# Attention scores by pairs of query tiles, with the second term as two 64-row products in the array's halves

## The chip, the cores and the metric

The kernel runs on one core of one Trainium2 chip. The metric is device time in microseconds of one execution. The time before is the median of three runs. Five engines work side by side, each with its own queue in program order: PE (TensorE, the 128 x 128 array), DVE (VectorE), ACT (ScalarE), POOL (GpSimd) and SP (SyncE), which only issues transfers. They wait for each other by semaphores.

## The reference

One decoder block over 2048 tokens of width 1024, in float32. What matters here is the mixer's attention: eight heads of width 64, strictly causal, in query tiles of 128.

```python
z = jnp.einsum('bhqd,bhkd->bhqk', qb, kb) * inv_sqrt
mask = s_idx < t_idx
log1m = jnp.where(mask, -jax.nn.softplus(z), 0.0)
after = lax.cumsum(log1m, axis=3, reverse=True) - log1m
logw = jax.nn.log_sigmoid(z) + after
w = jnp.where(mask, jnp.exp(jnp.where(mask, logw, 0.0)), 0.0)
outs.append(jnp.einsum('bhqk,bhkd->bhqd', w, vb))
```

Around it stand a conditioning product, a norm, one input projection (q, k, v and the pooling channels u), a causal pooling mixer, the output projection, and a dense SwiGLU layer.

## The kernel before, in words

**Precision.** Each operand of a product is split into a high and a low part in the fast float32r type: `split` casts on ACT (L58) and subtracts on DVE or POOL (L59). A product is then the sum of the terms high x high, high x low and low x high (`mm3`, L68 to L70).

**Stages.** First conditioning and the first projections; then attention, into which the rest of the projections is woven; then the output projection (`mix`), and the dense layer to the end, which is PE's alone.

**The attention's units.** A unit is (head h, query block tb, key block sc), both blocks of 512 tokens. There are 8 x 10 = 80 units; 32 have sc = tb (the diagonal). A unit has 4 steps, one for each query tile i of 128. A diagonal unit's step covers L = (i + 1) x 128 keys, all others 512. So there are 320 steps, 192 of them with 512 keys in 48 full units.

**A step's work, in order.** `weights_step` multiplies the tile's queries with the keys into z, one of two banks z0 and z1. The tile `qt` holds q's high part in both halves of the 128 rows, and q's low part likewise; `kt` holds k's high part in rows 0 to 63 and its low part in rows 64 to 127. So one 128-row product with `qt[:, 0]` gives high x (high + low) (L795), a second with `qt[:, 1]` gives low x (high + low) (L796). ACT makes two sigmoids of z, sg (L798) and pr (L800). `scan_step` runs a product scan over pr on DVE from the right (L811, `begin` holds the masks) and multiplies sg by it on POOL to give w (L817), with small copies of the carry (L808 to L815). `turn_step` transposes a unit's four w by key block b on PE into a bank wt (L828), casts it on ACT (wth, L58) and subtracts on DVE (wtl, L59). `values_step` multiplies both parts with the values (L843, L844) into one bank `av`; at a query block's end ACT copies it out (o, L848) and SP stores it.

**What sets the order.** PE, ACT, DVE and POOL run in the order in which this Python loop issues; SP's order is set by the framework's scheduler. Iteration n of the loop does: `values_step` of the turn three iterations back (LAG); `weights_step` of step n; `scan_step`, one a turn of the loop, if more than one is listed in `scans`; `turn_step` of step n - 7 (OFF); then filler pieces, as many as a pace sets that counts 4.0 for a full step and 2.5 for a diagonal one. A filler piece is three products of a projection (L68 to L70); every ninth piece is empty. 192 of the 226 pieces lie in the attention stage. With `block_loads` SP loads a block's q, k and v tiles (L777 to L779).

Of the kernel before, what the change touches and what calls it, by code (L numbers as in the profile page):

```python
# [10 lines left out]
F32R = mybir.dt.float32r  # L11
# [6 lines left out]
P = 128  # L18
# [5 lines left out]
DH = 64  # L24
# [4 lines left out]
TB = 512  # L29
# [14 lines left out]
def block_kernel(ctx, tc, x, c, w_cond, b_cond, g_mix_pre, g_mix_post, w_in, w_pool,  # L44
                 pool_scale, w_out, g_ffn_pre, g_ffn_post, w_gate, w_up, w_down, out):
    nc = tc.nc
# [6 lines left out]
    def raw(ap):  # L53
        return ap.bitcast(F32)
# [17 lines left out]
    def open_pool(stack, name, bufs=1, side=None):  # L72
        kw = {"side": side} if side else {}
        return stack.enter_context(tc.tile_pool(name=name, bufs=bufs, reuse_waits="tile", **kw))
# [4 lines left out]
    def dt(name, shape):  # L79
        return dram.tile(shape, F32, tag=name, name=name)  # L80

    qd = [[dt(f"qd{i}_{tb}", [2, P, TB]) for tb in range(NTB)] for i in range(4)]
    kd = [[dt(f"kd{i}_{tb}", [2, P, TB]) for tb in range(NTB)] for i in range(4)]
# [68 lines left out]
    def bank_cycle(*tags):  # L152
        tags = itertools.cycle(tags)
        return lambda name: psum(next(tags), 1, name)

    z_ps, t_ps, av_ps, mm_only = bank_cycle("z0", "z1", "z2"), bank_cycle("w0", "w1"), bank_cycle("a0", "a1"), bank_cycle("mm")
# [608 lines left out]
    qkp = open_pool(ph1, "qk", bufs=2)  # L765
    kv = {}

    def block_loads(h, tb):
        hp, j = h // 2, h % 2
        r = slice(j * DH, (j + 1) * DH)  # L770
        kt = qkp.tile([P, TB], F32R, tag="kt", bufs=6, name=f"kt{h}_{tb}")
        vt = att.tile([P, 4, P], F32R, tag="vt", bufs=6, name=f"vt{h}_{tb}")
        kv[h, tb] = kt, vt
        qt = qkp.tile([P, 2, TB], F32R, tag="qt", name=f"qt{h}_{tb}")
        for l in range(2):
            half = slice(l * DH, (l + 1) * DH)
            nc.sync.dma_start(raw(qt[half]), qd[hp][tb][:, r, :].rearrange("l d t -> d l t"))  # L777
            nc.sync.dma_start(raw(kt[half]), kd[hp][tb][l, r, :])
        nc.sync.dma_start(raw(vt), vd[tb][:, h, :].rearrange("(b p) e -> p b e", p=P))  # L779
        return qt  # L780

    qts, carries, avs, wss = {}, {}, {}, {}

    scans = []

    def weights_step(u, i):

        h, tb, sc = u
        diag = sc == tb
        kt, qt = kv[h, sc][0], qts[h, tb]  # L790
        L = (i + 1) * P if diag else TB
        nm = f"{h}_{tb}_{sc}_{i}"
        z = z_ps(f"z{nm}")
        keys = kt[:, 0:L]
        nc.tensor.matmul(z[:, 0:L], qt[:, 0, i * P:(i + 1) * P], keys, start=True, stop=False)  # L795
        nc.tensor.matmul(z[:, 0:L], qt[:, 1, i * P:(i + 1) * P], keys, start=False, stop=True)  # L796
        sg = att.tile([P, TB], F32, tag="sg", bufs=5, name=f"sg{nm}")
        nc.scalar.activation(sg[:, 0:L], z[:, 0:L], AF.Sigmoid, scale=0.125)  # L798
        pr = att.tile([P, TB + 1], F32, tag="pr", bufs=PRB, name=f"pr{nm}")
        nc.scalar.activation(pr[:, 0:L], z[:, 0:L], AF.Sigmoid, scale=-0.125)  # L800
        scans.append((u, i, pr, sg, L, nm))

    def scan_step(u, i, pr, sg, L, nm):

        diag = u[1] == u[2]
        carry = carries.pop(i, None)
        if carry is None:
            nc.gpsimd.memset(pr[:, L:L + 1], 0.0)  # L808
        else:
            nc.gpsimd.tensor_copy(pr[:, L:L + 1], carry)  # L810
        nc.vector.tensor_tensor_scan(pr[:, 0:L][:, ::-1], pr[:, 0:L][:, ::-1], begin[:, TB - L:][:, ::-1],  # L811
                                     zero if carry is None else carry, ALU.mult, ALU.max if diag else ALU.bypass)
        if u[2]:
            carries[i] = att.tile([P, 1], F32, tag=f"carry{i}", bufs=2, name=f"carry{nm}")
            nc.gpsimd.tensor_copy(carries[i], pr[:, 0:1])  # L815
        w = att.tile([P, TB], F32, tag="w", bufs=OFF + 4, name=f"w{nm}")
        nc.gpsimd.tensor_tensor(w[:, 0:L], sg[:, 0:L], pr[:, 1:L + 1], ALU.mult)  # L817
        wss.setdefault(u, []).append(w)

    def turn_step(u, b):  # L820

        h, tb, sc = u
        i0 = b if sc == tb else 0
        lo0 = i0 * P
        nm = f"{h}_{tb}_{sc}_{b}"
        wt = t_ps(f"wt{nm}")
        for i in range(i0, 4):
            nc.tensor.transpose(wt[:, i * P:(i + 1) * P], wss[u][i][:, b * P:(b + 1) * P], ident)  # L828
        wh = att.tile([P, TB], F32R, tag="wth", bufs=4, name=f"wth{nm}")
        wl = att.tile([P, TB], F32R, tag="wtl", bufs=4, name=f"wtl{nm}")  # L830
        split(wh[:, lo0:], wl[:, lo0:], wt[:, lo0:])
        return wh, wl, lo0

    def values_step(u, b, wh, wl, lo0):
        h, tb, sc = u
        hp, j = h // 2, h % 2
        first = sc == tb and b == 0
        last = sc == 0 and b == 3
        if first:
            avs[h, tb] = av_ps(f"av{h}_{tb}")  # L840
        av = avs[h, tb]
        vb = kv[h, sc][1][:, b, :]
        nc.tensor.matmul(av[:, lo0:], vb, wh[:, lo0:], start=first, stop=False)  # L843
        nc.tensor.matmul(av[:, lo0:], vb, wl[:, lo0:], start=False, stop=last)  # L844
        if last:
            end = (h, tb) == (HEADS - 1, NTB - 1)
            o1 = (up if end else wsp).tile([P, TB], F32, tag="um" if end else "o1", bufs=1, name=f"o1_{h}_{tb}")
            nc.scalar.copy(o1, av)  # L848
            for part, dst in enumerate((mtd, mld)):
                (nc.scalar if end else nc.sync).dma_start(dst[tb][hp, j * DH:(j + 1) * DH, :], o1[part * DH:(part + 1) * DH])  # L850

    def unit_loads(u):
        h, tb, sc = u
        if sc == tb:
            qts[h, tb] = block_loads(h, tb)
# [29 lines left out]
    z_ps, t_ps, av_ps, mm_only = bank_cycle(*('z0', 'z1')), bank_cycle(*('w0', 'w1', 'a1')), bank_cycle(*('a0',)), bank_cycle(*('mm',))  # L885
    steps = [(u, i) for u in units for i in range(4)]

    def wo_load():
        nonlocal wo_next
        for l in range(2):  # L890
            nc.sync.dma_start(raw(wo[wo_next][l]), wod[wo_next][l])
        wo_next += 1
# [20 lines left out]
    def mix_add(T, m32, l32):  # L913
        nc.gpsimd.tensor_tensor(m32[:, 0:HK], m32[:, 0:HK], l32, ALU.add)
        return T, m32
# [9 lines left out]
    def mix_products(T, mh, ml):  # L925
        pss = []
        for nh in range(2):
            cs2 = slice(nh * TB, (nh + 1) * TB)
            pss.append(f_ps(f"mix{T}_{nh}"))
            for k in range(KC):  # L930
                mm3(pss[nh], [((mh[:, k, :], ml[:, k, :]), (wo[k][0][:, cs2], wo[k][1][:, cs2]))],
                    first=k == 0, last=k == KC - 1)
                yield
        mixed[T] = pss
# [16 lines left out]
    for n in range(len(steps) + OFF):  # L951
        if len(waiting) > LAG:
            values_step(*waiting.pop(0))
        if n < len(steps):
            u, i = steps[n]
            if i == 0:
                unit_loads(u)
            weights_step(u, i)
            spent += 2.5 if u[1] == u[2] else 4.0
        if len(scans) > 1 or n >= len(steps) and scans:  # L960
            scan_step(*scans.pop(0))
        if n >= OFF:
            u, b = steps[n - OFF]
            waiting.append((u, b, *turn_step(u, b)))
        goal = START + (N_PIECES - START) * spent / (4 * sum(area[:END]))
        while fill is not None and taken < goal:
            taken += 1
            if next(fill, 0) == 0:
                fill = None
        for pool, here in ((hb, not wo and taken >= HB_FREE), (ha, len(wo) == 4 and fill is None)):  # L970
            if here:
                hi, lo = (pool.tile([P, 4, D], F32R, tag=tag, name=f"wo_{pool.name}{tag}")
                          for tag in ("hi", "lo"))
                wo.extend((hi[:, k, :], lo[:, k, :]) for k in range(4))
        if wo_next < len(wo):
            wo_load()
        if n in FIRST_LOADS:
            firsts.append(mix_load(SEQUENCE[FIRST_LOADS.index(n)]))
        if n in FIRST_SPLITS:
            products.append(mix_products(*mix_split(*firsts.pop(0))))  # L980
        if n in FIRST_ADDS:
            firsts[0] = mix_add(*firsts[0])
        if n >= len(steps):
            mix_pieces(PER_STEP)
# [592 lines left out]
```

## Time and profile before

| | us |
|---|---|
| median of three runs | 2325.14 (2323.5 to 2328.67) |
| the profiled execution | 2330.08 |
| its span, first to last instruction | 2328.3 |
| attention stage, first score product to last scan | 323.6 to about 840 |

The mean granted TensorE clock is 0.990. A line of a view names the engine, the line of the program, the operation, what is written `<-` what is read, and the form. Starts and durations of PE overlap, since products are pipelined: the distance from start to start tells what one costs. In a list of waits the three numbers are the total in us, how often, and the longest.

### The profile page before, as it was taken

To read this page: it belongs to the slowest core of one execution; us is meant where nothing else is said; L and a number is where in the kernel's file an instruction comes from. 1 tells how busy PE (TensorE), PEld (TensorE's weight loads), DVE (VectorE), ACT (ScalarE), POOL (GpSimd) and SP (SyncE) were. 2 spreads that over 40 slices of the span, in tenths; PEclk is the share of its full clock that TensorE was granted. 3 is DMA by queue.
4 is the path that set the end of the run, shared out by engine and by line. 5 is a ranking of instruction groups with operands and counts; after the bars stand their busy time and mean duration, and the time that the engine had idled before them with its cause. 6 is when DMAs were issued, how large, how long until landed. Compare 5 with 4: busy or idle time off the path is not lost.

```text
span 2328.3 us, 33054 instructions
## 1 busy us (share of the span) xinstructions
PE 2260.6 (97%) x10589; PEld 1854.3 (80%) x10589; DVE 1629.2 (70%) x2222; ACT 1163.5 (50%) x2411; POOL 1317.6 (57%) x1619
## 2 busy tenths in 40 slices
PE   6999999999999999999999999999999999999997
PEld 4778778888888777887888888888888888888885
DVE  6764549999999966756666565887766556565556
ACT  4323649899999854444323232554533323234444
POOL 4541337787778954555787878331476665641004
PEclk9999999999999999999999999999999999999998
DMA  8785764343435536655545555876754333328554
GB/s 286 257 288 193 259 210 119 99 111 91 128 105 164 161 111 195 213 193 181 171 154 163 158 159 181 272 247 214 257 172 128 99 113 91 114 91 285 189 195 145
DMA packets 307115, 405.15 MB, mean 174 GB/s; under 512 B 19254, under 2 KB 179578, under 8 KB 303868
## 3 DMA queue, kind: packets, MB, share of 16 engines
q1 hardware_dynamic: 302620, 400.68, 53.7%
q10 hardware_dynamic: 4320, 2.36, 0.4%
q8 instruction: 83, 1.36, 0.2%
q14 instruction: 92, 0.75, 0.1%
HBM read 274.51 MB, written 128.45 MB: 173 GB/s over the span
## 4 chain that ended last, share of the span: by engine, by line
PE 81%; DVE 6%; DMA 4%; POOL 4%; issue 3%; ACT 2%; SPq 0%; POOLq 0%; DVEq 0%; ACTq 0%
PE wt L828 4%; PE t_u L70 3%; PE t_u L68 3%; PE t_u L69 3%; PE t_g L69 3%; PE t_g L68 3%; PE t_g L70 3%; PE dn0p L69 3%; PE dn0p L70 3%; PE dn0p L68 3%; PE dn1p L69 3%; PE dn1p L68 3%; PE dn1p L70 3%; PE av L843 3%; PE av L844 2%
## 5 line engine op out<-in xcount | busy, mean ns | idle before, releaser
L817 POOL TENSOR_TENSOR w<-sg,pr 128x512 f32<-128x512 f32 (+2 forms) x320 | 307.3, 960 | 39.8 <-DVE pr L811 21.6
L1177 POOL TENSOR_TENSOR s<-s,cu 128x512 f32<-128x512 f32 x88 | 132.5, 1512 | 238.2 <-DVE cu L1176 145.8
L811 DVE TENSOR_TENSOR_SCAN pr<-pr,carry,begin 128x512 f32<-128x512 f32 x192 | 244.4, 1273 | 0.0
L798 ACT ACTIVATE sg<-z 128x512 f32<-128x512 f32 (+2 forms) x320 | 182.0, 569 | 49.6 <-PE z L796 35.5
L59 DVE TENSOR_TENSOR wtl<-wt,wth 128x512 fp32r<-128x512 f32 (+1 forms) x320 | 189.8, 593 | 20.5 <-ACT wth L58 19.6
L58 ACT CAST wth<-wt 128x512 fp32r<-128x512 f32 (+1 forms) x320 | 181.3, 567 | 13.0 <-PE wt L828 13.0
L800 ACT ACTIVATE pr<-z 128x512 f32<-128x512 f32 (+2 forms) x320 | 181.4, 567 | 0.0
L828 PE MATMUL wt<-ident,w 128*128 128x128 f32 x1088 | 173.9, 274 | 4.7 <-POOL w L817 2.3
L59 DVE TENSOR_TENSOR u_s_l<-u_s,u_s_h 128x512 fp32r<-128x512 f32 x66 | 65.4, 991 | 150.6 <-ACT u_s_h L58 150.6
L828 PEld LDWEIGHTS wt<-ident,w 128*128 128x128 f32 x1088 | 134.8, 141 | 35.4 <-POOL pr L808 3.2
L1167 ACT ACTIVATE s<-s 128x512 f32<-128x512 f32 x88 | 55.7, 633 | 192.0 <-DVE s L1166 192.0
L843 PE MATMUL av<-wth,vt 128*128 128x512 f32 (+1 forms) x320 | 129.9, 406 | 6.4 <-ACT o L848 6.3
L69 PE MATMUL dn0p<-w0p_l,g0p_h 128*128 128x512 f32 x308 | 121.0, 393 | 0.4 <-DVE w0p_l L59 0.4
L68 PE MATMUL dn0p<-w0p_h,g0p_h 128*128 128x512 f32 x308 | 120.6, 392 | 0.0
L70 PE MATMUL dn0p<-w0p_h,g0p_l 128*128 128x512 f32 x308 | 120.5, 391 | 0.0
L59 DVE TENSOR_TENSOR u_a_l<-u,u_a_h 128x512 fp32r<-128x512 f32 x66 | 76.2, 1156 | 62.7 <-ACT u_a_h L58 62.7
L844 PE MATMUL av<-wtl,vt 128*128 128x512 f32 (+1 forms) x320 | 118.5, 370 | 1.5 <-DVE wtl L59 1.3
L795 PE MATMUL z<-kt,qt 128*128 128x512 f32 (+2 forms) x320 | 117.6, 368 | 1.7 <-ACT pr L800 1.5
L58 ACT CAST g_s_h<-g_s 128x512 fp32r<-128x512 f32 x66 | 39.5, 620 | 157.6 <-POOL g_s L1109 80.7
L796 PE MATMUL z<-kt,qt 128*128 128x512 f32 (+2 forms) x320 | 117.1, 366 | 0.0
L69 PE MATMUL dn1p<-w1p_l,g1p_h 128*128 128x512 f32 x292 | 114.5, 392 | 0.0
L68 PE MATMUL dn1p<-w1p_h,g1p_h 128*128 128x512 f32 x292 | 114.3, 392 | 0.0
(652 smaller groups left out, 7184.5 us busy)
## 6 DMA issues: line engine op xcount, KB each, us to landing
g<-in_w_gate_dram SPq DMA_DIRECT2D x42, 512.0 KB, 5.0
u<-in_w_up_dram SPq DMA_DIRECT2D x42, 512.0 KB, 5.2
wc<-in_w_cond_dram SPq DMA_DIRECT2D x32, 512.0 KB, 5.7
qt<-qd SPq DMA_DIRECT2D x64, 256.0 KB, 3.9
wd<-in_w_down_dram SPq DMA_DIRECT2D x44, 256.0 KB, 2.9
tdt<-wd SPq DMA_DIRECT2D x44, 256.0 KB, 2.0
w0p<-tdt SPq DMA_DIRECT2D x44, 256.0 KB, 3.9
w1p<-tdt SPq DMA_DIRECT2D x44, 256.0 KB, 2.9
```

The costliest lines, as they stand in the source:

```text
L58: nc.scalar.copy(hi, src)
L59: low.tensor_tensor(lo, src, raw(hi), ALU.subtract)
L68: nc.tensor.matmul(ps, lh, rh, start=first and i == 0, stop=False)
L69: nc.tensor.matmul(ps, lh, rl, start=False, stop=False)
L70: nc.tensor.matmul(ps, ll, rh, start=False, stop=last and i == n - 1)
L798: nc.scalar.activation(sg[:, 0:L], z[:, 0:L], AF.Sigmoid, scale=0.125)
L800: nc.scalar.activation(pr[:, 0:L], z[:, 0:L], AF.Sigmoid, scale=-0.125)
L811: nc.vector.tensor_tensor_scan(pr[:, 0:L][:, ::-1], pr[:, 0:L][:, ::-1], begin[:, TB - L:][:, ::-1], zero if carry is None else carry, ALU ...
L817: nc.gpsimd.tensor_tensor(w[:, 0:L], sg[:, 0:L], pr[:, 1:L + 1], ALU.mult)
L828: nc.tensor.transpose(wt[:, i * P:(i + 1) * P], wss[u][i][:, b * P:(b + 1) * P], ident)
L843: nc.tensor.matmul(av[:, lo0:], vb, wh[:, lo0:], start=first, stop=False)
L844: nc.tensor.matmul(av[:, lo0:], vb, wl[:, lo0:], start=False, stop=last)
```

## The change

The scores are made for two steps at once, in the iteration of the odd one (`scores_step`). Both tiles' first terms come first, 128 rows each, unchanged. Then come both second terms, of 64 rows each: low q x high k only. The even tile's uses rows 0 to 63 of `qt` and `kt`; the odd tile's uses rows 64 to 127 of `qt` and of a new tile `k2` that holds k's high part there. So the low x low term is left out, and the two second terms lie in different halves of the array and write different banks. `k2` takes one more load a block. The rest of `weights_step` (both sigmoids, the entry in `scans`) then runs for the even and the odd step. Everything else stands as it was.

```diff
         vt = att.tile([P, 4, P], F32R, tag="vt", bufs=6, name=f"vt{h}_{tb}")
-        kv[h, tb] = kt, vt
+        k2 = qkp.tile([P, TB], F32R, tag="k2", bufs=5, name=f"k2{h}_{tb}")
+        kv[h, tb] = kt, vt, k2
...
             nc.sync.dma_start(raw(kt[half]), kd[hp][tb][l, r, :])
+        nc.sync.dma_start(raw(k2[half]), kd[hp][tb][0, r, :])
         nc.sync.dma_start(raw(vt), vd[tb][:, h, :].rearrange("(b p) e -> p b e", p=P))
...
-    def weights_step(u, i):
+    def scores_step(u, i0):
 
         h, tb, sc = u
-        diag = sc == tb
-        kt, qt = kv[h, sc][0], qts[h, tb]
-        L = (i + 1) * P if diag else TB
-        nm = f"{h}_{tb}_{sc}_{i}"
-        z = z_ps(f"z{nm}")
-        keys = kt[:, 0:L]
-        nc.tensor.matmul(z[:, 0:L], qt[:, 0, i * P:(i + 1) * P], keys, start=True, stop=False)
-        nc.tensor.matmul(z[:, 0:L], qt[:, 1, i * P:(i + 1) * P], keys, start=False, stop=True)
+        kt, _, k2 = kv[h, sc]
+        qt = qts[h, tb]
+        pair = []
+        for i in (i0, i0 + 1):
+            L = (i + 1) * P if sc == tb else TB
+            z = z_ps(f"z{h}_{tb}_{sc}_{i}")
+            nc.tensor.matmul(z[:, 0:L], qt[:, 0, i * P:(i + 1) * P], kt[:, 0:L], start=True, stop=False)
+            pair.append((i, z, L))
+        for (i, z, L), keys, rows in zip(pair, (kt, k2), (slice(0, DH), slice(DH, P))):
+            nc.tensor.matmul(z[:, 0:L], qt[rows, 1, i * P:(i + 1) * P], keys[rows, 0:L], start=False, stop=True)
+        for a in pair:
+            weights_step(u, *a)
+
+    def weights_step(u, i, z, L):
+
+        nm = "_".join(map(str, (*u, i)))
         sg = att.tile([P, TB], F32, tag="sg", bufs=5, name=f"sg{nm}")
...
             if i == 0:
                 unit_loads(u)
-            weights_step(u, i)
+            if i % 2:
+                scores_step(u, i - 1)
```

The order changes on each engine. The rows below are of one place, units of head 1 and query block 3; in the names stand tb, sc, and i or b, then a buffer's number (`o` has head and tb, `av` tb alone). PE before:

```order
L843 MATMUL av_3_4622<-wth_3_3_0_4554,vt_3_4351 128x512
L844 MATMUL av_3_4622<-wtl_3_3_0_4555,vt_3_4351 128x512
L795 MATMUL z_3_1_2_4625<-kt_1_3821,qt_3_4352 128x512
L796 MATMUL z_3_1_2_4625<-kt_1_3821,qt_3_4352 128x512
L828 MATMUL wt_3_3_3_4638<-ident,w_3_3_3_4469 128x128
L843 MATMUL av_3_4622<-wth_3_3_1_4580,vt_3_4351 128x384
L844 MATMUL av_3_4622<-wtl_3_3_1_4581,vt_3_4351 128x384
L795 MATMUL z_3_1_3_4646<-kt_1_3821,qt_3_4352 128x512
L796 MATMUL z_3_1_3_4646<-kt_1_3821,qt_3_4352 128x512
L828 MATMUL wt_3_2_0_4659<-ident,w_3_2_0_4496 128x128
```

PE after (`k_1` is the tile k2):

```order
L853 MATMUL av_3_4632<-wth_3_3_0_4564,vt_3_4361 128x512
L854 MATMUL av_3_4632<-wtl_3_3_0_4565,vt_3_4361 128x512
L838 MATMUL wt_3_3_3_4641<-ident,w_3_3_3_4506 128x128
L853 MATMUL av_3_4632<-wth_3_3_1_4583,vt_3_4361 128x384
L854 MATMUL av_3_4632<-wtl_3_3_1_4584,vt_3_4361 128x384
L797 MATMUL z_3_1_2_4649<-kt_1_3827,qt_3_4363 128x512
L797 MATMUL z_3_1_3_4651<-kt_1_3827,qt_3_4363 128x512
L800 MATMUL z_3_1_2_4649<-kt_1_3827,qt_3_4363 128x512
L800 MATMUL z_3_1_3_4651<-k_1_3829,qt_3_4363 128x512
L838 MATMUL wt_3_2_0_4669<-ident,w_3_2_0_4526 128x128
```

The score products of two iterations stand together ahead of the odd iteration's transposes; the even iteration has none. ACT before:

```order
L798 ACTIVATE sg_3_1_2_4628<-z_3_1_2_4625 128x512
L800 ACTIVATE pr_3_1_2_4630<-z_3_1_2_4625 128x512
L58 CAST wth_3_3_3_4640<-wt_3_3_3_4638 128x128
L798 ACTIVATE sg_3_1_3_4649<-z_3_1_3_4646 128x512
L800 ACTIVATE pr_3_1_3_4651<-z_3_1_3_4646 128x512
L58 CAST wth_3_2_0_4664<-wt_3_2_0_4659 128x512
```

ACT after:

```order
L58 CAST wth_3_3_3_4643<-wt_3_3_3_4641 128x128
L808 ACTIVATE sg_3_1_2_4655<-z_3_1_2_4649 128x512
L810 ACTIVATE pr_3_1_2_4657<-z_3_1_2_4649 128x512
L808 ACTIVATE sg_3_1_3_4659<-z_3_1_3_4651 128x512
L810 ACTIVATE pr_3_1_3_4661<-z_3_1_3_4651 128x512
L58 CAST wth_3_2_0_4674<-wt_3_2_0_4669 128x512
```

The four sigmoids of a pair stand in a row, ahead of the odd iteration's cast. DVE before:

```order
L811 SCALAR_TENSOR_TENSOR pr_3_1_1_4598<-pr_3_1_1_4598,carry_3_2_1_4521,begin 128x512
L59 TENSOR_TENSOR wtl_3_3_3_4641<-wt_3_3_3_4638,wth_3_3_3_4640 128x128
L811 SCALAR_TENSOR_TENSOR pr_3_1_2_4630<-pr_3_1_2_4630,carry_3_2_2_4545,begin 128x512
L59 TENSOR_TENSOR wtl_3_2_0_4665<-wt_3_2_0_4659,wth_3_2_0_4664 128x512
L811 SCALAR_TENSOR_TENSOR pr_3_1_3_4651<-pr_3_1_3_4651,carry_3_2_3_4572,begin 128x512
L59 TENSOR_TENSOR wtl_3_2_1_4689<-wt_3_2_1_4683,wth_3_2_1_4688 128x512
```

DVE after:

```order
L821 SCALAR_TENSOR_TENSOR pr_3_1_0_4604<-pr_3_1_0_4604,carry_3_2_0_4524,begin 128x512
L59 TENSOR_TENSOR wtl_3_3_3_4644<-wt_3_3_3_4641,wth_3_3_3_4643 128x128
L821 SCALAR_TENSOR_TENSOR pr_3_1_1_4608<-pr_3_1_1_4608,carry_3_2_1_4555,begin 128x512
L59 TENSOR_TENSOR wtl_3_2_0_4675<-wt_3_2_0_4669,wth_3_2_0_4674 128x512
L821 SCALAR_TENSOR_TENSOR pr_3_1_2_4657<-pr_3_1_2_4657,carry_3_2_2_4575,begin 128x512
L59 TENSOR_TENSOR wtl_3_2_1_4692<-wt_3_2_1_4686,wth_3_2_1_4691 128x512
```

Beside the same subtraction stands the scan of one step earlier: every scan has moved one iteration later, and with it POOL's product w.

## The prediction

> **What bounds the kernel now.** I first read the page's busy shares and the head of its chain, then the stage that the change touches, by windows. The attention stage runs from the first score product at 324 us to the last scan at about 840 us.
>
> ```profile
> span 2328.3 us, 33054 instructions
> ...
> PE 2260.6 (97%) x10589; PEld 1854.3 (80%) x10589; DVE 1629.2 (70%) x2222; ACT 1163.5 (50%) x2411; POOL 1317.6 (57%) x1619
> ...
> PE 81%; DVE 6%; DMA 4%; POOL 4%; issue 3%; ACT 2%; SPq 0%; POOLq 0%; DVEq 0%; ACTq 0%
> ```
>
> ```profile
> core 0: us, PE busy (x) PEld busy (x) DVE busy (x) ACT busy (x) POOL busy (x), PEclk, DMA share, GB/s
> 324.00:840.00 516.00, 501.72 (x2829) 416.44 (x2828) 500.39 (x648) 464.50 (x1057) 416.04 (x906) 1.00 0.44 124
> ```
>
> Over the whole program PE is the engine; in this stage DVE is as full as PE: it idles only 516.0 - 500.4 = 15.6 us. To see which of the two is really full, I read the timeline of one stretch with full tiles.
>
> ```profile
> 560.00 0.39 PE L795 MATMUL z<-kt,qt 128*128 128x512 f32 x1
> ...
> 560.23 0.39 PE L796 MATMUL z<-kt,qt 128*128 128x512 f32 x1
> ...
> 560.46 0.60 PE L828 MATMUL wt<-ident,w 128*128 128x128 f32 x4
> 560.51 1.27 DVE L811 TENSOR_TENSOR_SCAN pr<-pr,carry,begin 128x512 f32<-128x512 f32 x1
> ...
> 560.82 0.48 PE L68 MATMUL k<-hth,wk_h 128*128 128x512 f32 x1
> 560.85 0.67 ACT L798 ACTIVATE sg<-z 128x512 f32<-128x512 f32 x1
> ...
> 561.34 0.68 ACT L800 ACTIVATE pr<-z 128x512 f32<-128x512 f32 x1
> ...
> 561.59 0.39 PE L843 MATMUL av<-wth,vt 128*128 128x512 f32 x1
> ...
> 561.70 0.67 DVE L59 TENSOR_TENSOR wtl<-wt,wth 128x512 fp32r<-128x512 f32 x1
> 561.82 0.68 ACT L58 CAST wth<-wt 128x512 fp32r<-128x512 f32 x1
> ...
> 562.05 1.09 POOL L817 TENSOR_TENSOR w<-sg,pr 128x512 f32<-128x512 f32 x1
> ...
> 562.28 1.27 DVE L811 TENSOR_TENSOR_SCAN pr<-pr,carry,begin 128x512 f32<-128x512 f32 x1
> 562.28 0.39 PE L796 MATMUL z<-kt,qt 128*128 128x512 f32 x1
> ...
> 562.77 0.60 ACT L798 ACTIVATE sg<-z 128x512 f32<-128x512 f32 x1 [0.27 <-PE z L796]
> ```
>
> ```profile
> L828 PE MATMUL wt<-ident,w 128*128 128x128 f32 x1088 | 173.9, 274 | 4.7 <-POOL w L817 2.3
> ```
>
> Durations overlap, so I count from start to start. A 512-column product takes 0.23 us of PE (560.00 to 560.23), not its 0.39; a transpose 0.11, since four take 0.60 and one 0.27, so a turn takes 0.44; ACT spends 0.49 an operation; DVE spends 1.19 on a scan and 0.58 on a subtraction, 1.77 us a step without a hole; a sigmoid that waits starts 0.10 after its product's end (562.67 to 562.77). Summed so, PE streams in this stage: 1088 transposes at 0.11 = 119 us; score and value products, 278,528 columns each (8 heads x 17,408 columns x 2 terms) at 0.23 per 512 = 125 us each; fillers, 192 pieces of which 8 in 9 hold three products, 171 x 0.69 = 118. That is 487 of 516 us. So DVE (500) is the tighter engine and PE follows at 94%, whatever its busy share says. A gain on PE alone can win at most DVE's 15.6 us of idle time.
>
> Who waits now, in this stage:
>
> ```profile
> ACT sg L798 <- PE z L796: 35.5, 76, 2.6
> ...
> DVE wtl L59 <- ACT wth L58: 19.6, 34, 2.3
> PEld av L843 <- ACT o L848: 13.7, 24, 1.2
> ...
> PE av L843 <- ACT o L848: 6.3, 12, 1.0
> ...
> PE wt L828 <- POOL w L817: 2.3, 3, 1.1
> ```
>
> DVE's holes are waits for ACT's cast; PE almost never waits for POOL's product w.
>
> **Part 1, the products.** Per pair of steps four products stay four, but the second two are of 64 rows, in two halves of the array. What overlap is worth is bounded by the spacing: a full pair now spends 2 x 0.23 on its second terms; overlapped, 0.23 + d, with d the lag of the second behind the first. No row shows two halves at work. But the prologue shows changes of the array's shape: products with one column of weights between 128-column transposes.
>
> ```profile
> 19.74 1.09 PE L529 MATMUL x_pt<-ident,early_hi 128*128 128x128 f32 x8
> 20.76 1.88 PE L549 MATMUL am<-wc,cs 128*1 128x512 f32 x4
> 22.57 1.09 PE L529 MATMUL x_pt<-ident,early_hi 128*128 128x128 f32 x8
> ```
>
> ```profile
> L549 PE MATMUL am<-wc,cs x16: 590/592/1057, 12.9 to 24.9; 128*1 128x512 f32 x16
> ```
>
> There and back takes 22.57 - 19.74 = 2.83 us. Inside a group, products of L549 stand (1.88 - 0.59) / 3 = 0.43 apart, and transposes 0.11: 4 x 0.43 + 8 x 0.11 = 2.60. So two changes of shape cost 0.23 us, as much as a full pair's overlap can save. The Trainium skill, "TensorEngine Tiling (Array Packing)", section Tiling Modes, says that a change of tiling mode drains the engine, which speaks against a gain here; by that rule, the trace agrees, with its 0.23 us.
>
> For d the ends are 0 (both start together) and 0.23 (one after the other). I take 0.11, the closest that any two products stand in these rows (the transposes), since each half still has weights of its own to load. The Trainium skill, "TensorE: Matmul & The Clock Gate", Part 3, lets products in different row groups start some 4 ns apart; by that rule d is 0 and PE's part below is 6 us instead of 23.
>
> Full pairs, 96: 0.23 + 0.11 - 0.23 = +0.11 each, 10.6 us. Pairs of 384 and 512 columns, 32: overlap saves only 0.17, so +0.17 each, 5.4 us. Pairs of 128 and 256, 32: the 0.12 saved goes to the lag, so +0.23 each, 7.4 us. PE gets 23 us more, not less (ends: 6 with d = 0, 37 with none overlapping): 510 of 516. DVE hides much of it; a third counts, **+8 us** (ends 0 and 23).
>
> **Part 2, the scan comes a step later.** Scans are popped one a step once more than one is listed. Steps now arrive by twos, so the scan of a step runs two iterations after it instead of one (the order of DVE in the section on the change). The transposes of a unit still come seven iterations after its first step. So its last w has one iteration less, 1.77 us, before PE needs it.
>
> **Part 3, four sigmoids in a row.** On ACT the cast of odd iterations now stands behind four sigmoids, 1.96 us, instead of two, 0.98; on even ones behind none.
>
> Both meet in one loop. Let S be the start of the scan of a unit's last step. Its w ends at 562.05 + 1.09 - 560.51 = S + 2.63 us. Then, now: last transpose 0.16; values, transposes, values 0.46 + 0.44 + 0.46; the pair until its first sigmoid 1.07 (first terms 0.46, half the change of shape 0.12, a product's length 0.39, 0.10); four sigmoids 1.96; cast 0.63: S + 7.8, plus 0.69 for each filler piece between. DVE comes to that subtraction by its own work at S + 4 x 1.77 + 1.19 = S + 8.27. Before, the same path was 0.16 + 1.82 + 0.72 + 0.98 + 0.63 behind w, S + 6.94, and DVE's own time S + 5 x 1.77 + 1.19 = S + 10.04. The slack falls from 3.1 us to 0.5 us, and a filler piece takes 0.69. The pace gives full units about 1.3 pieces per two iterations: 7 in 10 have one (0.23 us late), 3 in 10 two (0.92 late), mean 0.4 us. A delay also delays DVE's own arrival a unit later, so half counts: 48 full units x 0.2 = **+10 us** (ends 0 and 20).
>
> Where a unit with small scans follows, DVE arrives sooner.
>
> ```profile
> L811 DVE TENSOR_TENSOR_SCAN pr<-pr,zero,begin x128: 455/868/1279, 325.9 to 816.7; 128x128 f32<-128x128 f32 x32, 128x256 f32<-128x256 f32 x32, 128x384 f32<-128x384 f32 x32, 128x512 f32<-128x512 f32 x32
> ```
>
> ```profile
> L811 DVE TENSOR_TENSOR_SCAN pr<-pr,zero,begin 128x256 f32<-128x256 f32 x32 | 23.6, 738 | 0.0
> ```
>
> The small scans take 0.46 and 0.74, 0.08 less from start to start. DVE is at the next unit's subtraction at S + 1.19 + 0.58 + 0.38 + 0.58 + 0.65 = S + 3.38. The shortest way for w is 2.63 + 0.05 + 0.27 (a transpose) + 0.04 + 0.63 = S + 3.62. That is 0.24 us late at each of 31 such places (four a head): **+7 us** (ends 0, if these holes exist already, and 15).
>
> **Part 4, the copy of the values.** PE waits 13.7 + 6.3 = 20 us for ACT to empty the one value bank. That copy falls at the head of an odd iteration, and ACT's iteration before it now holds only a cast: it starts up to 0.98 us sooner. A quarter of 20: **-5 us** (ends 0 and -15.6, DVE's idle time).
>
> **Part 5, loads.** 32 more loads of 128 KB on SP.
>
> ```profile
> kt<-kd SPq DMA_DIRECT2D x60, 128.0 KB, 2.6
> ```
>
> They land in 2.6 us, the DMA engines are at 0.44, and k2's tile is taken a block or more ahead: nothing. If that cover is gone, the first pair of a block is 2.6 us late, 32 times at most. Behind them on SP stand the q loads and the stores of o, which have a unit's time. The end: the last scan runs an iteration later, at most 1.8 us, beside products of the mix; nothing.
>
> **Sum.** 8 + 10 + 7 - 5 = +20 us. The profiled execution took 2330.1 us (span 2328.3): 2350. The median of the runs, 2325.1, is 5 us lower: **2345 us**.
>
> **Rivals.** (a) The halves overlap and the change of shape is hidden: the second terms save 0.23, 0.17 and 0.11 a pair, 31 us of PE. This is what the stage's high PE share would ask for. Then the pair is complete sooner, the loop has slack again, and the gain is capped by DVE's 15.6 us; half of it gives 2317 us. It decides if a pair's last first term and the next transposes start no more than 0.5 us apart (0.23 + 0.23; I expect 0.8). The 0.23 us of the prologue speak against it. The rule of the Trainium skill's "TensorE: Matmul & The Clock Gate", Part 3, leads to this case where nothing is paid at the change of shape; no run here shows it yet. (b) The change doesn't do what it says: the halves run one after the other. PE then has 487 + 37 = 524 us to stream, and with its 20 us at the value bank 544 in a stage of 516: +28, with the 7 of the small units 2360 us. Nothing in the trace excludes it. (c) PE merely falls back once by a step and the slack is spent without a hole: only 7 - 5 and little of PE's part, 2327 us. For it: PE had 29 us that it did not stream.
>
> **How the numbers follow.** The forecast 0.47 (its own range 2332 to 2358), (a) 0.18, (b) 0.20, (c) 0.15. A measurement of this kernel can tell 0.2%, 4.7 us. Faster comes from (a), 0.18; the same from (c), 0.15; slower 0.67 from the forecast and (b). The range 2319 to 2367 leaves out half of (a) and a third of (b).
>
> **What would show it.** Right: the start of a pair's second half about 0.1 us behind the first, and 0.8 us from the last first term to the transposes; DVE's waits for the cast grow from 19.6 us to over 35; PE's waits for w from 2.3 us to over 15; PE's waits for o fall; DVE's busy time stays about 500 while the stage ends near 860. Wrong: DVE's waits for the cast not above 20 us, or a stage that ends by 840.

## The result, and the profile after

The changed kernel takes **2392.5 us** (median of four runs, 2387.6 to 2397.4), the kernel before 2326.9 us beside it. The ratio is 1.0283, with a 95% interval of 1.0255 to 1.0311: 65.6 us slower. The direction was forecast; the size was not (2345 us, with 2367 us as the range's upper end).

The page of the changed kernel, its first lines and the head of its chain:

```profile
span 2388.3 us, 33089 instructions
...
PE 2295.9 (96%) x10589; PEld 1817.8 (76%) x10589; DVE 1636.8 (69%) x2222; ACT 1165.4 (49%) x2411; POOL 1315.9 (55%) x1619
...
PE 74%; DVE 9%; POOL 5%; ACT 4%; issue 4%; DMA 3%; SPq 0%; POOLq 0%; DVEq 0%; ACTq 0%
```

Busy time on PE rose by 35 us, less than the 60 us by which the span grew, and PE's share of the chain fell from 81% to 74%; DVE, ACT, POOL and "issue" took it. So the end is set more by waits than it was. By windows (columns as in the prediction):

```profile
324.00:840.00 516.00, 487.59 (x2563) 347.37 (x2562) 450.03 (x579) 416.51 (x951) 369.41 (x810) 1.00 0.40 113
324.00:910.00 586.00, 549.41 (x2873) 391.09 (x2872) 510.77 (x655) 468.95 (x1064) 418.44 (x909) 0.99 0.41 116
910.00:2300.00 1390.00, 1380.71 (x6114) 1136.18 (x6113) 882.61 (x1196) 527.25 (x1004) 743.19 (x534) 1.00 0.54 176
```

DVE was busy for 500 of the 516 us up to 840 before, and is busy for 450 now. The distance from the first score product to the last scan's end grew from 517 to 579 us, so the whole loss lies in the attention stage. Its waits, in the same form as before (total, times, longest):

```profile
ACT sg L808 <- PE z L800: 81.8, 108, 1.6
...
DVE wtl L59 <- ACT wth L58: 73.1, 89, 2.6
PEld z L800 <- issue: 42.1, 129, 0.4
...
PEld wt L838 <- issue: 25.8, 106, 0.2
...
PEld wt L838 <- POOL w L827: 21.2, 30, 2.4
...
PE wt L838 <- POOL w L827: 13.9, 19, 2.2
PE wt L838 <- POOL pr L818: 13.2, 18, 1.4
...
PEld av L853 <- ACT o L858: 3.8, 8, 0.9
```

DVE's waits for the cast went from 19.6 to 73.1 us, and PE's waits for w in the row `POOL w` from 2.3 to 13.9. The row `POOL pr L818` is the same wait under another name: a transpose reads only w and `ident`, and each of the 18 that this row counts starts 0.06 us after the end of a product w, as those of the row `POOL w` do. One of them, with POOL's w ending at 562.16 + 1.09 = 563.25:

```profile
562.16 1.09 POOL L827 TENSOR_TENSOR w<-sg,pr 128x512 f32<-128x512 f32 x1 [1.02 <-ACT sg L808]
563.19 0.10 POOL L818 MEMSET pr<- 128x1 f32 x1
...
563.30 0.33 PE L838 MATMUL wt<-ident,w 128*128 128x128 f32 x1 [1.29 <-POOL pr L818]
```

The same row of the kernel before:

```profile
PE wt L828 <- POOL pr L808: 2.3, 3, 1.2
```

So PE's waits for w went from 4.6 to 27.1 us. Those for the value bank all but went: the products' from 6.3 us to 1.6, by the page's group of that line, and their weight loads' from 13.7 to 3.8.

```profile
L853 PE MATMUL av<-wth,vt 128*128 128x512 f32 (+1 forms) x320 | 129.0, 403 | 1.8 <-ACT o L858 1.6
```

New are two rows in which the weight loads of the halves, and of the transposes behind them, wait for "issue". One stretch of the timeline shows both troubles:

```profile
567.19 0.61 ACT L808 ACTIVATE sg<-z 128x512 f32<-128x512 f32 x1
...
567.66 0.62 ACT L810 ACTIVATE pr<-z 128x512 f32<-128x512 f32 x1
...
568.14 1.11 ACT L58 CAST wth<-wt 128x512 fp32r<-128x512 f32 x2
...
568.62 0.63 PE L797 MATMUL z<-kt,qt 128*128 128x512 f32 x2
568.79 0.69 DVE L59 TENSOR_TENSOR wtl<-wt,wth 128x512 fp32r<-128x512 f32 x1 [1.13 <-ACT wth L58]
...
569.18 0.50 PE L800 MATMUL z<-kt,qt 64*128 64x512 f32 x1
...
569.18 0.50 PE L800 MATMUL z<-k,qt 64*128 64x512 f32 x1
...
569.61 0.66 PE L838 MATMUL wt<-ident,w 128*128 128x128 f32 x4
```

The two halves start together, at 569.18. Around them stand gaps: the pair's second first term starts at 568.62 + 0.63 - 0.39 = 568.86, the halves 0.32 us later instead of 0.23, and the transposes 0.43 us behind the halves instead of 0.23. The change back delays the second transpose too: it starts 0.165 us behind the first instead of 0.108 (medians over the full pairs of this kernel and over the full steps before), so a group of four takes 0.66 us instead of 0.60. And the cast behind the pair's sigmoids comes 1.13 us too late for DVE.

### The profile page after: what moved, and what is told of

Same layout as the page of the kernel before. It is cut to its first block, busy times and chain, and to the rows that moved or that the text cites. A ratio compares the mean times of both kernels' runs of the same rounds, so it can differ in the third digit from the quotient of the medians.

```text
span 2388.3 us, 33089 instructions
## 1 busy us (share of the span) xinstructions
PE 2295.9 (96%) x10589; PEld 1817.8 (76%) x10589; DVE 1636.8 (69%) x2222; ACT 1165.4 (49%) x2411; POOL 1315.9 (55%) x1619
## 4 chain that ended last, share of the span: by engine, by line
PE 74%; DVE 9%; POOL 5%; ACT 4%; issue 4%; DMA 3%; SPq 0%; POOLq 0%; DVEq 0%; ACTq 0%
PE t_u L70 3%; PE t_u L68 3%; PE t_u L69 3%; PE t_g L69 3%; PE t_g L68 3%; PE wt L838 3%; PE t_g L70 3%; DVE pr L821 3%; PE dn0p L69 3%; PE dn0p L70 3%; PE dn0p L68 3%; PE dn1p L68 3%; PE dn1p L69 3%; PE dn1p L70 3%; PE b_g L69 2%
## 5 line engine op out<-in xcount | busy, mean ns | idle before, releaser
L808 ACT ACTIVATE sg<-z 128x512 f32<-128x512 f32 (+2 forms) x320 | 177.0, 555 | 92.4 <-PE z L800 81.8
L838 PE MATMUL wt<-ident,w 128*128 128x128 f32 x1088 | 191.3, 284 | 27.5 <-POOL w L827 13.9
L838 PEld LDWEIGHTS wt<-ident,w 128*128 128x128 f32 x1088 | 126.2, 141 | 88.6 <-issue 25.8
L58 ACT CAST wth<-wt 128x512 fp32r<-128x512 f32 (+1 forms) x320 | 167.4, 575 | 26.4 <-PE wt L838 25.7
L70 PE MATMUL dn1p<-w1p_h,g1p_l 128*128 128x512 f32 x292 | 114.1, 391 | 0.0
L58 ACT CAST u_s_h<-u_s 128x512 fp32r<-128x512 f32 x66 | 38.6, 614 | 151.0 <-POOL u_s L1120 151.0
```

What stands on the lines that cost most here:

```text
L58: nc.scalar.copy(hi, src)
L70: nc.tensor.matmul(ps, ll, rh, start=False, stop=last and i == n - 1)
```

## The experiments

The change bundles four things: the 64-row halves with their changes of shape, the order of PE's products by pairs, four sigmoids in a row on ACT, and the scan one iteration later. Low x low is computed in every kernel below whose second terms are full rows of 128, and left out where they are of 64 rows.

### The scan's turn given back

```diff
-        if len(scans) > 1 or n >= len(steps) and scans:
+        if scans:
```

With that the changed kernel's scan stands one iteration behind its step, as before.

> The change with every scan back one iteration after its step's own iteration, as before; the pairs, the 64-row halves and the four sigmoids in a row stay. Theory A (the time went to the later w: scan and w one iteration later, met by the short scans of a diagonal unit): 2340 us, DVE's waits for the cast back from 73 to about 30 us and PE's waits for w from 28 (in the matmul rows) to about 5. Theory B (the array's changes of shape on PE): no more than 10 us better than the change, 2382 or more. Theory C (the four sigmoids in a row): 2375, since the cast of odd iterations still stands behind them.

2363.6 us, ratio 1.0156 (1.0141 to 1.0171): 29 us come back, but not the 52 that theory A wanted.

```profile
PEld z L800 <- issue: 42.0, 128, 0.5
...
DVE pr L821 <- ACT pr L810: 21.4, 46, 2.3
DVE wtl L59 <- ACT wth L58: 18.5, 35, 2.3
...
DVE pr L821 <- POOL pr L818: 4.7, 7, 0.8
```

DVE's waits for the cast are where they were before the change (18.5 us), so the 55 us by which they had grown do belong to the late scan. In their place DVE now waits 21.4 us for a sigmoid, and 4.7 us for POOL's small write into pr: the early scan follows its sigmoid too closely when four are made at once. The 55 less these 26 are the 29 us that come back.

### Full rows in the pair

```diff
...
+        for i, z, L in pair:
+            nc.tensor.matmul(z[:, 0:L], qt[:, 1, i * P:(i + 1) * P], kt[:, 0:L], start=False, stop=True)
```

The pair order stays, the halves and `k2` go.

> The change with second terms of 128 rows again (low x low back in, no k2 and no load of it), still by pairs, with scan and sigmoids as the change has them: the change of order alone. Theory A or C: 2375 to 2385 us, since only PE's extra 0.12 us a pair goes. Theory B: 2335 or less.

2377.4 us, ratio 1.0214 (1.0198 to 1.0229): the halves, with `k2`'s load, cost 15 us, and the larger part of the loss isn't in them. Both edits together:

> The change with 128-row second terms and with the scan back in its old iteration: what is left is the order by pairs on PE and the four sigmoids in a row on ACT. Theory A: 2330 to 2340 us. Theory C: 2365 or more. Theory B: 2330.

2345.3 us, ratio 1.0077 (1.0062 to 1.0092), some 5 us more than theory A expected. What is left, 19 us, is the price of the pair order alone. A pair's products in that kernel:

```profile
564.62 0.62 PE L795 MATMUL z<-kt,qt 128*128 128x512 f32 x2
565.08 0.63 PE L798 MATMUL z<-kt,qt 128*128 128x512 f32 x2
565.54 0.60 PE L836 MATMUL wt<-ident,w 128*128 128x128 f32 x4
```

From the first product to the transposes 0.92 us pass, against 569.61 - 568.62 = 0.99 with the halves, and the four transposes take 0.60 us against 0.66.

### The late scan by itself

```diff
-        if len(scans) > 1 or n >= len(steps) and scans:
+        if len(scans) > 2 or n >= len(steps) and scans:
```

This is the kernel before, with its products and sigmoids a step apiece.

> The kernel before with one thing changed: a scan is popped when more than two are listed, so that each runs two iterations after its step. Scores and sigmoids stay a step apiece. Theory A: 2350 to 2380 us, with PE's waits for w up from 2 us to over 15. Theory B or C: within 10 us of the kernel before.

2358.8 us, ratio 1.0136 (1.0119 to 1.0153): 32.7 us from this alone.

```profile
DVE wtl L59 <- ACT wth L58: 43.5, 85, 2.3
PEld wt L828 <- POOL w L817: 23.9, 32, 2.4
...
PE wt L828 <- POOL w L817: 16.2, 20, 2.2
```

The same two rows grow as in the changed kernel, without a pair and without a half. Then the transposes were moved an iteration later as well:

```diff
-OFF = 7
+OFF = 8
...
-        w = att.tile([P, TB], F32, tag="w", bufs=OFF + 4, name=f"w{nm}")
+        w = att.tile([P, TB], F32, tag="w", bufs=OFF + 3, name=f"w{nm}")
```

> The kernel before with the scan a step later (as in the run with the late scan alone, 2358.8 us) and the transposes a step later too (OFF = 8, w with OFF + 3 = 11 buffers, as many as before). Scores, sigmoids and their order stand as before. Theory: the late scan costs because the distance from w to the transposes that read it falls from 7 - 1 iterations to 7 - 2; given back here, the time returns to 2324 to 2335 us, PE waits under 5 us for w and DVE under 25 us for the cast. Rival: the late scan costs in another way (DVE's own order beside the cast, or the carry from unit to unit): 2345 us or more, with DVE's waits for the cast still about 40 us.

2333.2 us, ratio 1.0025 (1.0014 to 1.0035).

```profile
DVE wtl L59 <- ACT wth L58: 22.7, 38, 2.3
...
PE wt L828 <- POOL w L817: 3.4, 2, 1.8
```

25.6 of the 32.7 us are back, and both waits with them. Most of what the late scan costs is the distance from w to the transposes that read it.

### The same in the pair order: a miss, and its answer

The changed kernel with OFF = 8 and as many w buffers as it had:

> The change with the transposes of a unit eight iterations after its first step instead of seven, and the same 11 buffers of w. The scan stays late. If the loss of the late scan is the lost distance between w and its transposes: 2355 to 2368 us, as with the scan put back, PE's waits for w under 8 us. If the late scan costs by its own place on DVE: 2385 or more.

2397.4 us, ratio 1.0302 (1.0284 to 1.0319): nothing came back.

```profile
DVE wtl L59 <- ACT wth L58: 73.6, 92, 2.9
...
PEld av L853 <- ACT o L858: 41.3, 31, 2.5
PE av L853 <- ACT o L858: 31.2, 29, 2.3
```

PE's waits for w fell to 0.2 us, but a shift of one iteration trades odd for even: the copy o now stands behind four sigmoids, and PE waits 31 us for its bank. So that run couldn't answer the question. A shift of two keeps every turn on its side of the pair. It was tried in the kernel with full rows and the late scan, with 13 buffers of w:

```diff
-OFF = 7
+OFF = 9
```

> The kernel with pairs of full-row products and the late scan (2377.4 us), with the transposes two iterations later (OFF = 9, w with OFF + 4 = 13 buffers). Two, not one, so that the copy o and the turns keep their place in the pair. Low x low is computed. Theory: the late scan's price (32 us between this kernel and the one with the early scan, 2345.3 us) is the lost distance from w to the transposes, in the pair order as well: 2340 to 2352 us, DVE's waits for the cast fall from 67 us to under 30, PE's waits for w under 5. Rival: behind four sigmoids in a row the late scan costs in another way, as the turns one iteration later in the changed kernel (2397.4 us) might say: 2365 us or more, DVE's waits for the cast still above 50.

2351.6 us, ratio 1.0108 (1.0091 to 1.0125), against 2377.4 without the shift: 25.8 us back, as in the order of before.

```profile
DVE wtl L59 <- ACT wth L58: 38.1, 55, 2.3
...
PEld av L851 <- ACT o L856: 3.7, 4, 1.1
```

The cast's waits fell from 67.3 to 38.1 us, less than was expected (under 30), and PE's waits for w are gone. The lost distance is the main cause here too. The changed kernel itself, with its halves, was not run with a shift of two.

### What the pair order costs: ACT's part and PE's part

First ACT alone: products a step apiece, but both pairs of sigmoids made in the odd iteration, and the scan early.

```diff
+        ready.append((u, i, z, L, nm))
+        if i % 2:
+            while ready:
+                sigmoids(*ready.pop(0))
...
-        if len(scans) > 1 or n >= len(steps) and scans:
+        if scans:
```

> The kernel before with its products where they were, a step apiece, but the sigmoids of both steps of a pair made at the odd step, and each scan in its old iteration. So ACT's order is that of the run with 128-row second terms and early scans, and PE's is the old one. That run was 19 us over the kernel before. If those 19 us come from ACT's order (the scan of an even step now follows its sigmoid at once; four sigmoids ahead of a cast): 2338 to 2350 us, with DVE's scan waiting some 10 us for pr. If they come from PE's order (both first terms, then both second terms): within 6 us of the kernel before.

2333.8 us, ratio 1.0029 (1.0018 to 1.0039): 7.7 us, between the two expectations. Four sigmoids in a row cost something, but less than half of the 19 us. Then the reverse: PE's pair issued at the even step, with sigmoids and scans a step apiece as before.

```diff
...
+            if i % 2 == 0:
+                scores_step(u, i)
+            weights_step(u, *pairs.pop(0))
```

> 128-row second terms; the pair's products are issued at its even step, one step ahead for the odd tile, and sigmoids and scans run a step apiece, as before. ACT, DVE and POOL have their old order; only PE's differs. If ACT's order was the cause: 2322 to 2332 us. If PE's order is: 2338 or more, with PE waiting for ACT to free the second bank of z.

2362.5 us, ratio 1.0150 (1.0135 to 1.0165).

```profile
PEld z L795 <- ACT pr L807: 52.4, 98, 1.4
DVE wtl L59 <- ACT wth L58: 38.7, 94, 2.3
...
PE z L795 <- ACT pr L807: 20.2, 44, 1.1
```

The gain that ACT's theory promised isn't there. With two z banks, a pair's products made ahead wait until ACT has read the pair before. The same with halves:

> The same order with the 64-row second terms of the change (no low x low). Compared with the run with 128 rows in this call it prices the halves where nothing else is disturbed. By the change's own trace (a full pair 0.80 us from the last first term to the transposes against 0.68): PE gets some 20 us, DVE hides part of it, 8 to 18 us over that run. If the halves pay once the order is mended: 2320 or less.

2386.8 us, ratio 1.0257 (1.0242 to 1.0272): the halves cost 24 us in this order, more than the 8 to 18 that were expected.

### The price of the halves

The kernel before, with a second term of 64 rows alone:

```diff
-        nc.tensor.matmul(z[:, 0:L], qt[:, 1, i * P:(i + 1) * P], keys, start=False, stop=True)
+        nc.tensor.matmul(z[:, 0:L], qt[0:DH, 1, i * P:(i + 1) * P], keys[0:DH], start=False, stop=True)
```

> The kernel before with one edit: the second score term is a product of 64 rows (rows 0 to 63 of qt and kt), so low x low is left out, and nothing runs beside it. Order, scans and sigmoids stand as before; each of the 320 steps now holds two changes of the array's shape and no overlap. Theory: a change of shape costs what the changed kernel's rows show, 0.34 us for two (0.80 us from the last first term to the transposes, where two lengths of 0.23 would stand without it). PE then gets 320 x 0.34 = 109 us more, of which its 516 - 487 = 29 us that it doesn't stream can hide at most some: 2395 to 2435 us, with over 60 us of PE's weight loads waiting for issue at this line. Rival: the cost belongs to the halves (two products that start together and write two banks), and a 64-row product alone costs what a full one costs: 2322 to 2332 us.

2413.4 us, ratio 1.0376 (1.0360 to 1.0393): 86 us for changes of shape without any half beside.

```profile
558.65 0.39 PE L795 MATMUL z<-kt,qt 128*128 128x512 f32 x1
558.97 0.50 PE L796 MATMUL z<-kt,qt 64*128 64x512 f32 x1
559.40 0.55 PE L828 MATMUL wt<-ident,w 128*128 128x128 f32 x3
```

```profile
PEld z L796 <- issue: 91.1, 286, 0.4
...
PEld wt L828 <- issue: 51.6, 218, 0.2
```

A step takes 0.32 + 0.43 = 0.75 us where two full products take 0.46, so two changes cost 0.29 us up to the first transpose. With the second transpose, which starts 0.165 us behind the first instead of 0.108 here too, it is 0.35. The waits for issue stand at the two edges of the 64-row product; PE's other loads have 0.2 us of them in the whole stage.

Next, the changed kernel with both second terms in one half:

```diff
-        for (i, z, L), keys, rows in zip(pair, (kt, k2), (slice(0, DH), slice(DH, P))):
+        for (i, z, L), keys, rows in zip(pair, (kt, kt), (slice(0, DH), slice(0, DH))):
```

> The changed kernel with one edit: the odd tile's second term uses rows 0 to 63 as the even tile's does (kt in place of k2, whose load stays), so both 64-row products of a pair stand in one half of the array and cannot run at once; order and changes of shape stand. Theory: the halves did run at once in the changed kernel, so a pair's second half now starts 0.23 us (512 columns) behind the first, and PE gets 31 us more: 2402 to 2424 us. Rival: the 3 ns between the two starts in the trace are not what the work took, and the halves were never worth anything: 2387 to 2397 us, as the changed kernel.

2398.4 us, ratio 1.0311 (1.0296 to 1.0326): 6 us more than the changed kernel, between the two expectations, and hardly clear of the spread of the two kernels' runs (2387.6 to 2397.4 us, and 2396.3 to 2399.3 here).

```profile
570.77 0.68 PE L797 MATMUL z<-kt,qt 128*128 128x512 f32 x2
571.38 0.73 PE L800 MATMUL z<-kt,qt 64*128 64x512 f32 x2
572.04 0.33 PE L838 MATMUL wt<-ident,w 128*128 128x128 f32 x1
```

On PE it is as the theory said: the halves' part, from their start to the transposes, takes 0.66 us here and 0.43 in the changed kernel. The overlap is real and worth 0.23 us a full pair. In time little of it counts. One more run changes what the longer stretch delays, with the 64-row products ahead of the pair's 128-row products:

> The changed kernel with one edit: a pair's two 64-row products come first and its two 128-row products behind them. The same products, halves, changes of shape and orders of ACT and DVE; PE streams as long. Only the even tile's scores are complete sooner: in the changed kernel the first sigmoid starts 1.15 us after the pair's first product (568.62 to 569.77), and here by its rows 0.43 + 0.39 + 0.10 = 0.92 us, 0.1 of it more ahead of it: about 0.15 us sooner a pair, 160 times. Theory S: the halves' price is the later start of the four sigmoids, on the way to the cast: 2372 to 2384 us, as far as the kernel with full rows (2377.4). Theory P: the price is PE's longer stream: 2388 to 2397 us.

2392.0 us, ratio 1.0282 (1.0255 to 1.0308): as the changed kernel. Over all pairs the median from the pair's first product to its first sigmoid fell from 1.15 to 1.03 us, and the time is the same. PE's stream isn't quite as long as was meant: from the product ahead of a pair to the second transpose behind it 1.42 us pass by the median, against 1.38 in the changed kernel, some 7 us over 160 pairs. That could hide a gain of a few us, but hardly the 8 to 20 of theory S. The later start of the sigmoids isn't the main price.

## Why the prediction was right or wrong

**The sum.** The runs make a path from before to after: the pair order +19 (full rows, early scan), the late scan +32, the halves +15. The other edges are near: the late scan costs 32.7 us without the pair order and 28.9 with halves; the halves cost 18.3 with the early scan and 24.2 with the products made ahead. The forecast had 17 for the scan and the sigmoids (parts 2 and 3), 8 for the halves (part 1), -5 for the copy, and no term for PE's pair order. Three steps failed: the share of PE's extra work that counts (a third), the size of the late scan's price where a unit with small scans follows, and the order by pairs, which was priced through the sigmoids alone.

**Part 1.** Its sum on PE came out, but by luck: two of its terms were wrong in opposite ways. d is 0 and not 0.11 us: the starts lie 3 ns apart. The change of shape costs 0.35 us there and back, up to the second transpose, and not the 0.23 of the prologue, where the shape changes in its columns and not in its rows. Per full pair that makes 0.35 - 0.23 = +0.12 us, where +0.11 was forecast. By medians of all pairs, up to the second transpose and against the pairs of full rows with the late scan, the smaller ones have +0.17 (384 and 512 columns) and +0.24 (128 and 256), so PE got 96 x 0.12 + 32 x 0.17 + 32 x 0.24 = 25 us, where 23 were forecast. The step that failed is "a third counts": 15 to 24 us were measured for the halves, from 0.6 of it to nearly all. By the same medians the short rows alone gave PE 108 us, of which 86 counted. So 22 us were hidden there, and the prediction had PE not streaming for 516 - 487 = 29. That the single half gave PE 31 us more by medians and cost only some 6 us shows that the share isn't fixed; why it was so small there stays open.

**Parts 2 and 3.** The mechanism was right: the slack between w, the transposes, the cast and the subtraction. The late scan alone, the shift of the transposes and DVE's waits show it. Its size was wrong. The holes ahead of DVE's subtractions add up as follows (worked out from all instructions of both traces; the last unit, which none follows, has some 5 us of them in both):

| | before | after | more | forecast |
|---|---|---|---|---|
| next unit is full, or none | 9.6 us | 24.6 us | 15 | 10 |
| next unit has small scans | 10.9 us | 51.1 us | 40 | 7 |

That is 55 us more of holes, in a stage that grew by 62. The mis-sized term is "where a unit with small scans follows", 0.24 us at each of 31 places; measured are 40 / 31 = 1.3. The price was worked out with the shortest way for w, as if no product and no sigmoid stood in it. But a unit's first turn falls on an odd iteration, where the cast stands behind four sigmoids. And of the 51 us, 18.7 stand ahead of the unit's third turn, the next odd iteration, for which there was no term. Added up in the same way, the holes where a unit with small scans follows are 29 us with the late scan alone, 9 with the sigmoids by pairs alone, and 45 with the late scan and pairs of full rows; those ahead of the third turn are 1.6, 1.0 and 17.1. So the late w makes a part of the 40 us by itself, and the rest together with the four sigmoids ahead of the cast.

**The missing term.** That the order by pairs costs 19 us with full rows and the early scan was priced only through the sigmoids. These alone cost 7.7. The other 11 or so belong to PE's order, or to both together; no run split them further. The waits for z's two banks in the run with the products ahead show one way in which a pair order costs; that it is this in the changed kernel is not shown, since the row for it there is small:

```profile
PEld z L797 <- ACT pr L810: 11.6, 30, 0.8
```

**Part 4** had the right direction in the trace: PE's waits for the bank fell from 6.3 us to 1.6. But its 20 us count the same waits twice: the 6.3 us in which PE waits lie within the 13.7 of its weight loads (worked out from both rows' intervals), so there were 6.3 us to win. The same 20 stands in the 544 of rival (b). In time the gain isn't seen, since DVE's holes set the pace; no run tried it alone. **Part 5**: nothing in the waits speaks of k2's load; no run takes it away by itself, so it is part of what the halves are said to cost.

**The rivals.** (a) falls: the halves do overlap, but the change of shape isn't hidden; from the last first term to the transposes 0.75 us pass (568.86 to 569.61), not 0.5 and near the 0.8 expected. (b) falls: the halves don't run one after the other. (c) falls with DVE's waits. The Trainium skill, "TensorE: Matmul & The Clock Gate", Part 3, has products in different row groups start some 4 ns apart; the trace agrees, with 3 ns. The Trainium skill, "TensorEngine Tiling (Array Packing)", section Tiling Modes, says that a change of tiling mode drains the engine; the trace agrees, with 0.35 us for two changes.

**What would show it.** Right: DVE's waits for the cast over 35 us (73.1), the 0.8 us, the waits for o, and DVE's busy time (510.8 us). Nearly, in the row that it named: PE's waits for w, 13.9 where over 15 were expected; with the second row they are 27.1. Wrong: the lag of 0.1 us, and a stage that ends near 860; it ended at about 903.

No version here is faster than the kernel before.

## What to carry to other kernels

An overlap in the array's halves has to pay for the change of shape at both ends: 0.35 us here, more than the 0.23 us that two 512-column products save, so a pair set alone between full-height products loses. By an estimate from these rows it would take at least two such pairs in a row (2 x 0.23 saved against 0.35), which was not tried. When a reordering moves a producer one iteration, count the distance to every consumer, place by place, with the work that really stands in each queue there, not by the shortest way; and see whether the consumer can move too, which gave back 26 of 32 us here. A shift by one iteration in an order of period two also moves every other turn to the other side, so shift by the period.

## What was not expected of the hardware

Two 64-row products on different halves of the array started 3 ns apart (median over all pairs). The change of shape from 128 rows to 64 cost about 0.09 us and the way back about 0.20 (0.32 and 0.43 against 0.23), and another 0.06 in the distance from the first transpose behind it to the second. In both places the weight load, which elsewhere runs beside the product ahead of it, waited for issue (42.1 and 25.8 us in the changed kernel, where the kernel before has one such wait of 0.3 at its score products). A 64-row product of 512 columns is recorded with 0.49 to 0.50 us, a full one with 0.39.
